# Quarter sums by accumulating DMAs, shift dots on VectorE and filters beside the first stage's last projections: one DiT layer on one core

## Chip, core and metric

The program runs on one core of a Trainium2 chip. The metric is the device time of one execution in microseconds (us). TensorE (PE) multiplies, PEld loads its weights, VectorE (DVE) and ScalarE (ACT) do element work, GpSimd (POOL) does element work and issues DMAs of its own queue, SyncE (SP) issues all other DMAs.

## What is computed

One layer of a diffusion transformer on 512 latent and 256 context tokens of width 1024, all in fp32. `m` and `mc` are nine vectors each, from the conditioning `c` and `c_ctx`:

```python
m = jnp.split((jax.nn.silu(c) @ mod_w[l] + mod_b[l])[:, None, :], N_MOD, axis=-1)
mc = jnp.split((jax.nn.silu(c_ctx) @ mod_w[l] + mod_b[l])[None, None, :], N_MOD, axis=-1)
h = half_ffn(h, m[0], m[1], m[2], ffn_w_gate[l, 0], ffn_w_up[l, 0], ffn_w_down[l, 0])
hc = half_ffn(hc, mc[0], mc[1], mc[2], ffn_w_gate[l, 0], ffn_w_up[l, 0], ffn_w_down[l, 0])
n = modulate(rms_norm(h), m[3], m[4])
nc = modulate(rms_norm(hc), mc[3], mc[4])
...
s_fw, s_bw = context_states(nc, w_in[l], lb_all[l])
...
out, _, _ = token_mixers(n, s_fw, s_bw, hyena_kernels(n_lat, *filt_w), *mix_w)
h = h + m[5] * out
h = half_ffn(h, m[6], m[7], m[8], ffn_w_gate[l, 1], ffn_w_up[l, 1], ffn_w_down[l, 1])
return rms_norm(h) * final_norm_w
```

`half_ffn` is a gated feed-forward network (hidden width 2816) on the normed input, shifted and scaled by two of the vectors. `token_mixers` projects with `w_in`, runs a gated linear recurrence in four heads and two long convolutions ("Hyena"), whose filters a small network makes, and projects back.

## The kernel before

Every fp32 operand of a matmul is split into a rounded high part and a low rest (`split`: a CAST on ACT, a subtraction on DVE or POOL), and each product is three matmuls (high by high, low by high, high by low).

**First stage** (`ffn0`, the first `half_ffn`, latents and context together). The 22 tiles of the hidden width are worked in five groups (`GROUPS0`: 4, 4, 4, 4 and 6 tiles); below they are groups 0 to 4. Group 0 multiplies plainly. Before it can work on the context, `shifts` must make the shift columns `m0` of the latents and the context: for each of eight tiles of `mod_w` two dots over 512 elements for the latents and one over 1024 for the context. Groups 1 to 4 use a seven-product scheme for 2x2 blocks (`quads0`): the 512-column quarters `a11, a12, a21, a22` of two weight tiles and four sums of them, `s1 = a21+a22`, `s2 = s1+a11`, `s3 = a11+a21`, `s4 = a12+s2`, are split and multiplied in the order a11, s2, s3, s1, a12, a22, s4 (in PE's names p1, p6, p7, p5, p2, p4, p3). Two tiles of gate and up weights make two such "quads", 18 in all. After its products each group multiplies with `w_d` for eight column tiles (the down part); the partial results of groups 0 to 3 are summed in DRAM, group 0 with stores, the others with accumulating DMAs of POOL's queue (`y_dram`, `yc_dram`). The last group's down part (`ps_dl` for latents, `ps_dc` for the context) adds them up with the residual.

**Background.** `bg` runs beside groups 0 to 4, a step at a time (`adv(bg)`, two in each quad, one at each column tile of a down part). `mod_steps` makes the other modulation vectors from 56 tiles of `mod_w` of 512 KB, two buffers in turn: tile n+1 can be loaded only when the dots of tile n-1 are done. The first 24 tiles are heavy (two dots over 512 and one over 1024), the other 32 light (one dot over 1024).

**Mixers.** After the first stage, 52 projection tiles (`fill_all`) are the fill of PE. Generators with long chains on DVE and ACT, `context_norm`, `filters` (four), `convs` (four halves, `e` forward and `j` back transform) and the heads, are run against the fill by `Clock.run`, which by hand-given costs (us of PE, us of chain) decides which piece is recorded next.

**What sets the order.** Weights are loaded along a list (`plan`), some tiles being held for a second use (`hold`). The recorded program then goes through a scheduler which reorders instructions on each engine (`schedule_with_timeline_sim=True`). SP, POOL, DVE, ACT and PE each work in order: an instruction that waits holds up all behind it on its engine.

Of the kernel before, what the change touches and what calls it, by code (L numbers as in the profile page):

```python
# [10 lines left out]
F32 = mybir.dt.float32  # L11
# [84 lines left out]
def layer_kernel(ctx: ExitStack, tc: tile.TileContext, a: dict, out: bass.AP):  # L96
# [26 lines left out]
        return mx.tile([P] + dims, dt, tag="c4", name=name, bufs=8)  # L123

    def c2(name, dims, dt=F32):
        return mx.tile([P] + dims, dt, tag="c2", name=name, bufs=15)

    def c1(name, dims, dt=F32):
        return mx.tile([P] + dims, dt, tag="c1", name=name, bufs=6)
# [5 lines left out]
    def load(dst, src):  # L135
        nc.sync.dma_start(out=dst, in_=src)
# [8 lines left out]
    def raw_tile(name):  # L145
        return wp.tile([P, 1024], F32, tag="wraw", name=name, bufs=3)
# [5 lines left out]
    for g, (f0, f1) in enumerate(GROUPS0):  # L152
        if g == 0:
            gu = [(a[w][0, ft], 1024) for ft in range(f0, f1) for w in ("wg", "wu")]
            plan += hold(gu[:6], [RING] * 3 + [ONE8, RES2, TWO4]) + gu[6:]
        else:
            plan += [(a[w][0, ft], a[w][0, ft + 1], QUAD0) for ft in range(f0, f1, 2) for w in ("wg", "wu")]
        down = [(a["wd"][0, dm, :, f0 * P:f1 * P], (f1 - f0) * P) for dm in range(KT)]
        plan += hold(down, [RING] * 3 + [ONE8] * 2 + [RES2] + [RING] * 2) + down[0:3] if g == len(GROUPS0) - 1 else down
# [78 lines left out]

    def quads0(src0, src1):

        raws = []
        for src in (src0, src1):
            raws.append(raw_tile("wraw"))
            load(raws[-1], src)
        (a11, a12), (a21, a22) = (r.rearrange("p (h c) -> h p c", h=2) for r in raws)

        def total(x, y):
            t = c2("qs", [512])
            V.tensor_tensor(out=t, in0=x, in1=y, op=ALU.add)  # L249
            return t  # L250

        def both(x, eng=V):
            w = ("whi", "wlo")[wstate["slot"]]
            wstate["slot"] ^= 1
            t = wp.tile([P, 2, 512], F32R, tag=w, name=w, bufs=3)
            split(t[:, 0], t[:, 1], x, eng)
            return t[:, 0], t[:, 1], None

        yield both(a11, G)
        s1 = total(a21, a22)  # L260
        s2 = total(s1, a11)
        yield both(s2)
        yield both(total(a11, a21))
        yield both(s1)
        yield both(a12, G)
        yield both(a22, G)
        yield both(total(a12, s2))
# [117 lines left out]
    def dot(out_, raw, vec, res):  # L385
        return V.scalar_tensor_tensor(out=out_, in0=raw, scalar=1.0, in1=vec, op0=ALU.mult, op1=ALU.mult, accum_out=res)  # L386

    m_part = const.tile([P, KT], F32, name="m_part")

    def mod_steps():  # L390
        raw = [c4("wmod", [1024]) for _ in range(2)]
        tiles = [(j, dm) for j in range(2, 9) for dm in range(KT)]

        def fetch(i):
            if i < len(tiles):
                load(raw[i % 2], a["mod_w"][8 * tiles[i][0] + tiles[i][1]])

        fetch(0)
        yield
        for n, (j, dm) in enumerate(tiles):  # L400
            fetch(n + 1)
            col = j * 8 + dm
            r = raw[n % 2]
            if j < 5:
                junk = c2("junk", [512])
# [190 lines left out]

    def scale_columns(h):

        row = mx.tile([2, 512], F32, tag="c2", name="mrow", bufs=15)
        A.copy(row, p_scale[h][0:2, :])  # L600
        p_ = ps("ps_mt")
        for k in range(4):
# [4 lines left out]

    p_scale = []

    def pool_dot(raw, res):  # L610

        G.tensor_tensor(out=raw, in0=raw, in1=cvb[1], op=ALU.mult)
        A.activation(raw, raw, AF.Identity, accum_out=res)

    def shifts(kts):
        for kt in kts:
            junk = c2("junk", [512])
            for h, res in enumerate((m0[:, kt, 0:1], m_part[:, kt:kt + 1])):
# [289 lines left out]
    def ffn0():  # L908
        for gi, (f0, f1) in enumerate(GROUPS0):
            ml, mc = [], []  # L910
            if gi == 0:
                kept = [weights(6 - i) for i in range(6)]
                early = [ps("ps_gl") for _ in range(4)]
                for kt in range(KT):
                    if kt == 1:
                        accc = squares(hc, range(KT), c1, C, V)
                    if kt == 2:
                        shifts(range(4))
                    if kt == 5:
# [61 lines left out]
            if gi < len(GROUPS0) - 1:  # L981
                for dm in range(KT):
# [10 lines left out]
                continue  # L993

            def residual0(h_, y, p_, m, dm):
                V.tensor_tensor(out=y, in0=p_, in1=y, op=ALU.add)
                V.scalar_tensor_tensor(out=h_, in0=y, scalar=m[:, 16 + dm:17 + dm], in1=h_, op0=ALU.mult, op1=ALU.add)

            for _ in bg:
                pass  # L1000
            acc = norm["lat"]
            kept = []
            hl2 = [c8("hl", [4, L]) for _ in range(2)]
            yl = [c8("yl", [4, L]) for _ in range(2)]
            hc2, yc = (c8(x, [KT, C]) for x in ("hc", "yc"))
            for dm in range(0, KT, 2):
                i, ks = dm // 4, slice(dm % 4, dm % 4 + 2)
                load(hl2[i][:, ks], x0_dram[:, dm:dm + 2])
                load(yl[i][:, ks], y_dram[:, dm:dm + 2])
            load(hc2, a["ctxT"])  # L1010
            load(yc, yc_dram)
            nhi, nlo = (Halves([c8(x, [4, L], F32R) for _ in range(2)]) for x in ("nhi", "nlo"))
            for dm in range(KT):
                pl = ps("ps_dl")
                kept.append(weights(min(2, KT - dm)))
                down(kept[dm], lx, [pl])
                residual0(hk(hl2, dm), hk(yl, dm), pl, m_lat, dm)
                sq_add(acc, hk(hl2, dm), dm, c2, L)
                store(h_dram[:, dm], hk(hl2, dm))
            accc = norm["ctx"]  # L1020
            nl = norm_steps(acc, hl2, LS, nhi, nlo, m_lat, 3, 4, c2)
            for n, dm in enumerate((6, 7, 3, 4, 5, 0, 1, 2)):
                pc = ps("ps_dc")
                prefetch(1 if n == 0 else 2)
                down(weights() if n >= 5 else kept[dm], cx, [pc[:, 0:C]])
                if n >= 1:
                    adv(nl, 1 if n < 3 else 2)
                residual0(hc2[:, dm], yc[:, dm], pc[:, 0:C], m_ctx, dm)
                sq_add(accc, hc2[:, dm], n, c1, C)
# [135 lines left out]
            yield cost / 2, 1.4  # L1165

    def fill_all():
        for _ in range(52):
            prefetch()
            while not chosen:  # L1170
# [567 lines left out]
```

## Time and profile before

| | |
|---|---|
| device time, median of 3 runs (range) | 1596.77 us (1595.14 to 1599.26) |
| the profiled execution: its time, its span | 1599.4 us, 1597.4 us |
| mean granted clock of TensorE | 0.965 |
| busy PE, DVE, ACT, POOL | 1473.6, 1190.6, 634.5, 473.4 us |
| moved by DMA | 209.60 MB |

The span runs from the first instruction to the last. A busy share is an average over stages that have different limits, so the stages are read one by one: which engine is full there, and what PE waits for.

### The profile page before, as it was taken

The page shows a single profiled execution, that of the slowest core. Times are in us where ns is not written, and L with a number is a line of the kernel's source. Part 1 is how long each engine was busy: PE and PEld are TensorE (multiplying, and loading weights), DVE is VectorE, ACT ScalarE, POOL GpSimd, SP SyncE. Part 2 cuts the span into 40 slices and gives each one's busy share as a digit, 9 for nine tenths or more (in the row PEclk, how much of TensorE's full clock was granted, in tenths as well). Part 3 has the DMA queues.
Part 4 walks back from the last instruction along what each step waited for, and adds up shares of the span by engine and source line. Part 5 has one row for each costly group of instructions (what it writes and reads, how often), then busy time and mean ns, then how long its engine had stood idle before and what let it go on. Part 6 is the DMA issues. An engine that isn't in the chain of part 4 may idle for free.

```text
span 1597.4 us, 22680 instructions
## 1 busy us (share of the span) xinstructions
PE 1473.6 (92%) x8560; PEld 1312.8 (82%) x8560; DVE 1190.6 (75%) x1833; ACT 634.5 (40%) x1141; POOL 473.4 (30%) x350
## 2 busy tenths in 40 slices
PE   8779887999999999999999958998798999999997
PEld 4578886988989988887778847887688899989897
DVE  6768995986868968665447888777466678869687
ACT  5344332343434445434232423444433344535353
POOL 1221534445545510135754111211232011302020
PEclk9989998999999999999999989998799999999998
DMA  9306338449393183435333541114423042322422
GB/s 386 102 21 225 131 119 216 139 130 253 115 262 100 50 298 108 140 104 185 119 122 126 171 157 62 45 49 145 161 93 116 14 118 89 105 92 97 122 72 87
DMA packets 81805, 209.60 MB, mean 131 GB/s; under 512 B 9179, under 2 KB 22239, under 8 KB 81056
## 3 DMA queue, kind: packets, MB, share of 16 engines
q1 hardware_dynamic: 71856, 193.18, 36.0%
q0 software_dynamic: 8256, 13.78, 4.3%
q8 instruction: 67, 1.10, 0.3%
q10 hardware_dynamic: 1584, 1.20, 0.2%
q14 instruction: 42, 0.34, 0.1%
HBM read 175.88 MB, written 32.24 MB: 130 GB/s over the span
## 4 chain that ended last, share of the span: by engine, by line
PE 59%; DVE 22%; DMA 7%; issue 6%; ACT 3%; POOL 1%; SPq 0%; ACTq 0%; DVEq 0%; POOLq 0%
PE ps_w L310 5%; PE ps_w L313 5%; PE ps_w L311 5%; PE ps_p L313 4%; PE ps_p L310 4%; PE ps_p L311 4%; PE ps_dl L310 3%; PE ps_dl L311 3%; PE ps_dl L313 3%; DMA wmod<-in_mod_w 3%; DVE wlo L143 2%; DVE junk L386 2%; DVE wmod L386 2%; DVE qs L249 2%; DVE whi L143 2%
## 5 line engine op out<-in xcount | busy, mean ns | idle before, releaser
L142 ACT CAST whi<-wraw 128x512 fp32r<-128x512 f32 (+2 forms) x187 | 151.4, 810 | 299.1 <-issue 78.4
L143 DVE TENSOR_TENSOR wlo<-wraw,whi 128x1024 fp32r<-128x1024 f32 (+2 forms) x114 | 124.6, 1095 | 57.4 <-ACT whi L142 55.1
L310 PE MATMUL ps_w<-nhi,whi 128*128 128x512 f32 x352 | 143.5, 408 | 0.0
L313 PE MATMUL ps_w<-nhi,wlo 128*128 128x512 f32 x352 | 140.0, 398 | 3.7 <-DVE wlo L143 3.7
L311 PE MATMUL ps_w<-nlo,whi 128*128 128x512 f32 x352 | 140.1, 398 | 0.0
L313 PE MATMUL ps_dl<-mid,wlo 128*128 128x512 f32 (+1 forms) x318 | 122.2, 387 | 0.2 <-DVE wlo L143 0.2
L311 PE MATMUL ps_dl<-mid,whi 128*128 128x512 f32 (+1 forms) x318 | 122.1, 386 | 0.0
L310 PE MATMUL ps_dl<-mid,whi 128*128 128x512 f32 (+1 forms) x318 | 121.0, 388 | 0.2 <-ACT mid L142 0.2
L143 POOL TENSOR_TENSOR wlo<-wraw,whi 128x1024 fp32r<-128x1024 f32 x19 | 51.0, 2684 | 232.5 <-ACT whi L142 189.0
L1564 POOL TENSOR_TENSOR u<-p,res 128x512 f32<-128x512 f32 x18 | 33.0, 1833 | 283.9 <-ACT p L1559 140.6
L386 DVE SCALAR_TENSOR_TENSOR wmod<-wmod,cvb 128x1024 f32<-128x1024 f32 x56 | 73.5, 1313 | 24.6 <-DMA wmod<-in_mod_w 24.3
L313 PEld LDWEIGHTS ps_w<-nhi,wlo 128*128 128x128 f32 x352 | 66.9, 190 | 16.6 <-DVE wlo L143 4.2
L310 PEld LDWEIGHTS ps_w<-nhi,whi 128*128 128x128 f32 x352 | 67.3, 191 | 15.1
L311 PEld LDWEIGHTS ps_w<-nlo,whi 128*128 128x128 f32 x352 | 67.2, 191 | 11.5
L142 ACT CAST whi<-qs 128x512 fp32r<-128x512 f32 x72 | 44.3, 619 | 78.8 <-DVE qs L249 40.2
L143 DVE TENSOR_TENSOR whi<-qs,whi 128x512 fp32r<-128x512 f32 x72 | 67.4, 947 | 4.6 <-ACT whi L142 4.3
L143 DVE TENSOR_TENSOR wlo<-qs,wlo 128x512 fp32r<-128x512 f32 x72 | 58.1, 813 | 16.6 <-ACT wlo L142 15.9
L142 ACT CAST wlo<-qs 128x512 fp32r<-128x512 f32 x72 | 43.9, 619 | 66.3 <-DVE qs L249 41.5
L310 PEld LDWEIGHTS ps_dl<-mid,whi 128*128 128x128 f32 x318 | 59.5, 188 | 12.3 <-ACT mid L142 0.7
L143 POOL TENSOR_TENSOR wlo<-wraw,wlo 128x512 fp32r<-128x512 f32 x27 | 48.2, 1785 | 65.7 <-ACT wlo L142 58.3
L313 PEld LDWEIGHTS ps_dl<-mid,wlo 128*128 128x128 f32 x318 | 60.0, 189 | 7.5 <-DVE wlo L143 0.4
L311 PEld LDWEIGHTS ps_dl<-mid,whi 128*128 128x128 f32 x318 | 59.9, 188 | 7.3 <-DVE mid L143 0.2
(533 smaller groups left out, 4929.2 us busy)
## 6 DMA issues: line engine op xcount, KB each, us to landing
wmod<-in_mod_w SPq DMA_DIRECT2D x56, 512.0 KB, 3.5
wraw<-in_wg SPq DMA_DIRECT2D x44, 512.0 KB, 3.4
wraw<-in_wu SPq DMA_DIRECT2D x44, 512.0 KB, 3.4
wraw<-in_w_in SPq DMA_DIRECT2D x44, 512.0 KB, 3.3
wraw<-in_wd SPq DMA_DIRECT2D x35, 384.0 KB, 3.5
wraw<-in_wd SPq DMA_DIRECT2D x40, 256.0 KB, 3.0
wm<-in_mod_w SPq DMA_DIRECT2D x16, 512.0 KB, 10.2
y_dram<-yt POOLq DMA_DIRECT2D x24, 256.0 KB, 9.2
```

What stands on the lines that cost most here:

```text
L142: A.copy(hi, x)
L143: return eng.tensor_tensor(out=lo, in0=x, in1=hi.bitcast(F32), op=ALU.subtract)
L249: V.tensor_tensor(out=t, in0=x, in1=y, op=ALU.add)
L310: PE.matmul(o, whi, xhi, start=first, stop=False)
L311: PE.matmul(o, whi, xlo, start=False, stop=False)
L313: PE.matmul(o, wlo, xhi, start=False, stop=last)
L386: return V.scalar_tensor_tensor(out=out_, in0=raw, scalar=1.0, in1=vec, op0=ALU.mult, op1=ALU.mult, accum_out=res)
L1564: G.tensor_tensor(out=u57, in0=p57, in1=res[:, 1:2].broadcast_to([P, 2, 256]), op=ALU.add)
```

## The change

1. **Quarter sums.** In `quads0`, s1 and s3 are no longer made by DVE. SP loads one of the two terms into a tile `qs`, and a DMA of POOL's queue adds the other onto it (`accum_op=add`). a21 alone is no longer loaded; the loads of a quad are five of 256 KB on SP's queue and two accumulating ones of 256 KB on POOL's, in place of two of 512 KB.
2. **Shift dots.** All eight context dots of `shifts` are on DVE; before, six were a product on POOL and a sum on ACT. The Silu of the conditioning vectors `cvb` and the norm factors of the context (`rstd_steps`) are recorded earlier.
3. **Background tiles.** Of the first 48 tiles, heavy and light ones take turns.
4. **Last down part.** `ffn0_end` is a generator that is itself fill; `filters` run beside it from its first piece, `context_norm` once it is done. Five of its eight weight tiles are loaded twice, before three.
5. The scratch tile `junk` of the dots has a place of its own; the ring of 512-element tiles has 14 places, before 15.

```diff
     def quads0(src0, src1):
...
-        (a11, a12), (a21, a22) = (r.rearrange("p (h c) -> h p c", h=2) for r in raws)
+        a11, a12 = raw_tile("wraw").rearrange("p (h c) -> h p c", h=2)
+        k0, k1 = slice(0, 512), slice(512, 1024)
+        load(a11, src0[:, k0])
+        s1, s3 = (c2("qs", [512]) for _ in range(2))
+        for t, x, y in ((s1, src1[:, k0], src1[:, k1]), (s3, src0[:, k0], src1[:, k0])):
+            load(t, x)
+            nc.gpsimd.dma_start(out=t, in_=y, accum_op=ALU.add)
+        load(a12, src0[:, k1])
+        a22 = raw_tile("wraw")[:, 0:512]
+        load(a22, src1[:, k1])
...
-        s1 = total(a21, a22)
         s2 = total(s1, a11)
         yield both(s2)
-        yield both(total(a11, a21))
+        yield both(s3)
         yield both(s1)
...
         tiles = [(j, dm) for j in range(2, 9) for dm in range(KT)]
+        tiles = [tiles[i // 2 if i % 2 == 0 else 24 + i // 2] for i in range(48)] + tiles[48:]
...
-    def pool_dot(raw, res):
-
-        G.tensor_tensor(out=raw, in0=raw, in1=cvb[1], op=ALU.mult)
-        A.activation(raw, raw, AF.Identity, accum_out=res)
-
     def shifts(kts):
...
-            if kt in (0,1,3,4,5,7):
-                pool_dot(shift_w[kt], m0[:, kt, 1:2])
-            else:
-                dot(shift_w[kt], shift_w[kt], cvb[1], m0[:, kt, 1:2])
+            dot(shift_w[kt], shift_w[kt], cvb[1], m0[:, kt, 1:2])
...
-                    if kt == 5:
-                        for _ in rstd_steps([accc], C, "rc", rx):
-                            pass
+                    if kt == 2:
+                        stats = rstd_steps([accc], C, "rc", rx)
+                        adv(stats)
+                    if kt == 4:
+                        adv(stats, 2)
...
+    def ffn0_end(lx, cx):
...
+            store(h_dram[:, dm], hk(hl2, dm))
+            yield 4.1, 2.2
...
     def fill_all():
+        yield from ffn0_end(*ends)
         for _ in range(52):
...
-    ck.run([context_norm(), filters()], fill, lambda i: True, 2)
+    ck.run([filters(), context_norm()], fill, lambda i: i == 0 or "mixers" in state, 2)
```

**DVE ahead of the context's first products** (`wm` is a tile of `mod_w`, `m_part` the second halves of the latents' dots, `rr` the context's norm factors). Before:

```order
L143 TENSOR_TENSOR wkeep<-wraw,wkeep 128x1024 x2
L460 RECIPROCAL rr<-rr 128x2
L143 TENSOR_TENSOR wkeep<-wraw,wkeep 128x1024
L386 SCALAR_TENSOR_TENSOR junk,m_193<-wm_332,cvb 128x512
L386 SCALAR_TENSOR_TENSOR junk,m_193<-wm_334,cvb 128x512
```

Now:

```order
L143 TENSOR_TENSOR wkeep<-wraw,wkeep 128x1024 x2
L390 SCALAR_TENSOR_TENSOR junk,m_194<-wm_333,cvb 128x512
L390 SCALAR_TENSOR_TENSOR junk,m_part<-wm_333,cvb 128x512
L465 RECIPROCAL rr<-rr 128x2
L390 SCALAR_TENSOR_TENSOR wm_333,m_194<-wm_333,cvb 128x1024
L390 SCALAR_TENSOR_TENSOR junk,m_194<-wm_335,cvb 128x512
L467 TENSOR_TENSOR dg<-ident,rr 128x256
L143 TENSOR_TENSOR wkeep<-wraw,wkeep 128x1024
```

The first dots stand ahead of the context's norm factors, and each tile's context dot follows its two latent dots on the same engine.

**SP at the start of group 3** (its first quad reads two tiles of `in_wg`, the next two of `in_wu`). Before:

```order
L136 DMA wraw_3304<-in_wg 128x1024
L136 DMA wmod_1109<-in_mod_w 128x1024
L136 DMA wraw_3306<-in_wg 128x1024
L136 DMA wmod_1108<-in_mod_w 128x1024
L136 DMA wraw_3405<-in_wu 128x1024
```

Now:

```order
L136 DMA wraw_3277<-in_wg 128x512 x2
L136 DMA wmod_1095<-in_mod_w 128x1024
L136 DMA wraw_3286<-in_wg 128x512
L136 DMA wmod_1096<-in_mod_w 128x1024
L136 DMA wraw_3382<-in_wu 128x512 x2
L136 DMA wmod_1095<-in_mod_w 128x1024
L136 DMA wmod_1096<-in_mod_w 128x1024
L136 DMA qs_3279<-in_wg 128x512
L136 DMA qs_3280<-in_wg 128x512
```

The second tile of weights stood ahead of two background loads that stand ahead of s1's and s3's first terms now.

**DVE at the same place.** Before:

```order
L386 SCALAR_TENSOR_TENSOR wmod_1109,m_lat_96<-wmod_1109,cvb_328 128x1024
L249 TENSOR_TENSOR qs_3311<-wraw_3306 128x512
L249 TENSOR_TENSOR qs_3313<-qs_3311,wraw_3304 128x512
L143 TENSOR_TENSOR wlo_3315<-qs_3313,wlo_3315 128x512
L386 SCALAR_TENSOR_TENSOR wmod_1108,m_lat_96<-wmod_1108,cvb_328 128x1024
```

Now:

```order
L390 SCALAR_TENSOR_TENSOR wmod_1096,m_lat_96<-wmod_1096,cvb_329 128x1024
L254 TENSOR_TENSOR qs_3291<-qs_3279,wraw_3277 128x512
L254 TENSOR_TENSOR qs_3361<-wraw_3277,qs_3291 128x512
L143 TENSOR_TENSOR wlo_3293<-qs_3291,wlo_3293 128x512
L390 SCALAR_TENSOR_TENSOR junk_146,m_lat_96<-wmod_1095,cvb_329 128x512
```

s2 (`qs_3291`) follows the same light dot; what it reads, `qs_3279`, is now written by a load and an accumulating DMA.

**PE in the convolutions**, around the first two back transforms. Before:

```order
L313 MATMUL ps_e<-zhi,ft 128x256
L310 MATMUL ps_j<-it,ys 128x256
L311 MATMUL ps_j<-it,ys 128x256
L310 MATMUL ps_j<-it,ys 128x256
L311 MATMUL ps_j<-it,ys 128x256
L310 MATMUL ps_e<-zhi,ft 128x256
```

Now:

```order
L317 MATMUL ps_w<-nhi,wlo 128x512
L314 MATMUL ps_w<-nhi,whi 128x512
L315 MATMUL ps_w<-nlo,whi 128x512
L317 MATMUL ps_w<-nhi,wlo 128x512
L314 MATMUL ps_j<-it,ys 128x256
L315 MATMUL ps_j<-it,ys 128x256
```

The first back transform stood straight behind the forward transform that feeds it; now 114 matmuls of fill (`ps_w`) stand between the two. The second half's `j` stands straight behind its `e` in both.

## Rows read from the trace of the kernel before

**Rows 1.** The page's first part: busy time and share of each engine.
```profile
PE 1473.6 (92%) x8560; PEld 1312.8 (82%) x8560; DVE 1190.6 (75%) x1833; ACT 634.5 (40%) x1141; POOL 473.4 (30%) x350
```
**Rows 2.** Windows: stretch, length, busy PE, PEld, DVE, ACT, POOL (instructions), clock, DMA share, GB/s.
```profile
75.00:100.00 25.00, 11.98 (x76) 11.99 (x77) 13.93 (x27) 7.75 (x18) 8.96 (x6) 0.62 0.05 17
159.00:236.00 77.00, 68.02 (x374) 64.41 (x372) 76.83 (x123) 28.32 (x57) 34.98 (x23) 1.00 0.40 130
...
264.00:349.00 85.00, 69.58 (x374) 65.99 (x373) 76.51 (x113) 28.87 (x58) 36.96 (x25) 0.94 0.47 145
349.00:376.00 27.00, 27.00 (x156) 23.57 (x155) 13.55 (x25) 10.13 (x23) 13.44 (x15) 1.00 0.90 241
376.00:447.00 71.00, 68.06 (x375) 66.38 (x375) 61.95 (x83) 29.35 (x58) 37.58 (x26) 0.98 0.53 162
...
474.00:570.00 96.00, 93.21 (x511) 90.78 (x510) 79.94 (x110) 46.59 (x88) 50.05 (x39) 0.98 0.34 102
570.00:604.00 34.00, 33.65 (x149) 27.39 (x148) 22.82 (x34) 10.68 (x17) 0.00 (x0) 1.00 0.80 299
```
**Rows 3.** PE's waits: matmul, what it waited for, us in total, times, longest.
```profile
PE ps_j L310 <- ACT ys L142: 22.1, 3, 13.9
PE ps_gc L310 <- ACT bh L142: 18.2, 1, 18.2
PE ps_p L310 <- ACT wlo L142: 11.0, 1, 11.0
...
PE ps_w L313 <- DVE wlo L143: 3.7, 1, 3.7
```
**Rows 4.** DVE's timeline, 51 to 88 us: start, us, instruction, idle time before.
```profile
51.43 0.17 DVE L460 RECIPROCAL rr<-rr 128x2 f32<-128x2 f32 x1 [7.83 <-ACT rr L459]
...
54.74 0.69 DVE L386 SCALAR_TENSOR_TENSOR junk<-wm,cvb 128x512 f32<-128x512 f32 x1 [1.15 <-ACT cvb L663]
...
58.75 2.89 DVE L386 SCALAR_TENSOR_TENSOR junk<-wm,cvb 128x512 f32<-128x512 f32 x1
...
67.72 1.21 DVE L386 SCALAR_TENSOR_TENSOR wm<-wm,cvb 128x1024 f32<-128x1024 f32 x1
...
69.87 1.27 DVE L628 SCALAR_TENSOR_TENSOR mt<-hc,m,rc 128x256 f32<-128x256 f32 x3
...
87.56 0.17 DVE L932 TENSOR_TENSOR m<-m,sm 128x16 f32<-128x16 f32 x1 [3.48 <-ACT wm L613]
```
**Rows 5.** Groups by line, whole span: busy, mean ns, idle time before.
```profile
L249 DVE TENSOR_TENSOR qs<-wraw 128x512 f32<-128x512 f32 x36 | 39.6, 1101 | 4.5 <-DMA wraw<-in_wg 4.1 <-DMA wraw<-in_wu 0.5
...
L991 POOL DMA_DIRECT2D y_dram<-yt x24 | 24.5, 1021 | 55.1 <-ACT yt L987 54.7
```
**Rows 6.** Groups by line, DVE in 159 to 236 us.
```profile
L386 DVE SCALAR_TENSOR_TENSOR junk<-wmod,cvb 128x512 f32<-128x512 f32 x18 | 18.2, 1011 | 0.1
L386 DVE SCALAR_TENSOR_TENSOR wmod<-wmod,cvb 128x1024 f32<-128x1024 f32 x10 | 13.6, 1364 | 0.0
```
**Rows 7.** DMA queues (packets, MB, share), then issues: KB each, median us to landing.
```profile
q1 hardware_dynamic: 71856, 193.18, 36.0%
q0 software_dynamic: 8256, 13.78, 4.3%
...
wraw<-in_wg SPq DMA_DIRECT2D x44, 512.0 KB, 3.4
...
y_dram<-yt POOLq DMA_DIRECT2D x24, 256.0 KB, 9.2
...
k_dram<-te POOLq DMA_DIRECT2D x8, 256.0 KB, 3.8
```
**Rows 8.** Timeline of SP's queue at the start of group 3.
```profile
375.30 5.44 SPq L136 DMA_DIRECT2D wmod<-in_mod_w  x2
```
**Rows 9.** Timeline of PE at the start of group 3.
```profile
378.57 0.45 PE L310 MATMUL ps_p<-tt,wlo 128*128 128x386 f32 x1
...
384.18 0.69 PE L310 MATMUL ps_p<-tt,whi 128*128 128x386 f32 x1 [2.83 <-ACT whi L142]
```

More of the change, by code (lines that the diff above doesn't have):

```diff
@@ L125, in c2 @@
     def c2(name, dims, dt=F32):
-        return mx.tile([P] + dims, dt, tag="c2", name=name, bufs=15)
+        return mx.tile([P] + dims, dt, tag="c2", name=name, bufs=14)
     def c1(name, dims, dt=F32):
@@ L158, in layer_kernel @@
         down = [(a["wd"][0, dm, :, f0 * P:f1 * P], (f1 - f0) * P) for dm in range(KT)]
-        plan += hold(down, [RING] * 3 + [ONE8] * 2 + [RES2] + [RING] * 2) + down[0:3] if g == len(GROUPS0) - 1 else down
+        plan += hold(down, [RING] * 5 + [RES2] + [RING] * 2) + down[0:5] if g == len(GROUPS0) - 1 else down
     plan += [None] * 52
@@ L239, in quads0 @@
     def quads0(src0, src1):
[L241 to L244, printed above, removed]
-        (a11, a12), (a21, a22) = (r.rearrange("p (h c) -> h p c", h=2) for r in raws)
+        a11, a12 = raw_tile("wraw").rearrange("p (h c) -> h p c", h=2)
[8 more added lines that the diff above has]
+        load(a22, src1[:, k1])
         def total(x, y):
@@ L386, in dot @@
         return V.scalar_tensor_tensor(out=out_, in0=raw, scalar=1.0, in1=vec, op0=ALU.mult, op1=ALU.mult, accum_out=res)
+    junk = const.tile([P, 512], F32, name="junk")
     m_part = const.tile([P, KT], F32, name="m_part")
@@ L404, in mod_steps @@
             if j < 5:
-                junk = c2("junk", [512])
                 for h, res in enumerate((m_lat[:, col:col + 1], m_part[:, dm:dm + 1])):
@@ L597, in scale_columns @@
     def scale_columns(h):
-        row = mx.tile([2, 512], F32, tag="c2", name="mrow", bufs=15)
+        row = mx.tile([2, 512], F32, tag="c2", name="mrow", bufs=14)
         A.copy(row, p_scale[h][0:2, :])
@@ L608, in layer_kernel @@
     p_scale = []
-    def pool_dot(raw, res):
-        G.tensor_tensor(out=raw, in0=raw, in1=cvb[1], op=ALU.mult)
-        A.activation(raw, raw, AF.Identity, accum_out=res)
     def shifts(kts):
         for kt in kts:
-            junk = c2("junk", [512])
             for h, res in enumerate((m0[:, kt, 0:1], m_part[:, kt:kt + 1])):
@@ L659, in layer_kernel @@
     shift_w = rows(range(4), "wm0")
+    for i in range(2):
+        tc.keep_in_program_order(A.activation(cvb[i], cvb[i], AF.Silu))
     prefetch(6)
     shift_w += rows(range(4, KT), "wm0")
-    for i in range(2):
-        tc.keep_in_program_order(A.activation(cvb[i], cvb[i], AF.Silu))
     for i in range(2):
@@ L992, in ffn0 @@
                     adv(bg)
[L993 to L1029, printed above, removed]
@@ L1030, in ffn0, with residual0 @@
-            adv(nl, 8)
-        return nhi, nlo, hc2
+        return lx, cx
+    nhi = nlo = chi = clo = hc2 = lat_x = None
+    def ffn0_end(lx, cx):
+        nonlocal nhi, nlo, chi, clo, hc2, lat_x
+        def residual0(h_, y, p_, m, dm):
+            V.tensor_tensor(out=y, in0=p_, in1=y, op=ALU.add)
+            V.scalar_tensor_tensor(out=h_, in0=y, scalar=m[:, 16 + dm:17 + dm], in1=h_, op0=ALU.mult, op1=ALU.add)
+        for _ in bg:
+            pass
+        acc = norm["lat"]
+        kept = []
+        hl2 = [c8("hl", [4, L]) for _ in range(2)]
+        yl = [c8("yl", [4, L]) for _ in range(2)]
+        hc2, yc = (c8(x, [KT, C]) for x in ("hc", "yc"))
+        for dm in range(0, KT, 2):
+            i, ks = dm // 4, slice(dm % 4, dm % 4 + 2)
+            load(hl2[i][:, ks], x0_dram[:, dm:dm + 2])
+            load(yl[i][:, ks], y_dram[:, dm:dm + 2])
+        load(hc2, a["ctxT"])
+        load(yc, yc_dram)
+        nhi, nlo = (Halves([c8(x, [4, L], F32R) for _ in range(2)]) for x in ("nhi", "nlo"))
+        for dm in range(KT):
+            pl = ps("ps_dl")
+            kept.append(weights(min(2, KT - dm)))
+            down(kept[dm], lx, [pl])
+            residual0(hk(hl2, dm), hk(yl, dm), pl, m_lat, dm)
+            sq_add(acc, hk(hl2, dm), dm, c2, L)
+            store(h_dram[:, dm], hk(hl2, dm))
+            yield 4.1, 2.2
+        accc = norm["ctx"]
+        nl = norm_steps(acc, hl2, LS, nhi, nlo, m_lat, 3, 4, c2)
+        for n, dm in enumerate((6, 7, 5, 0, 1, 2, 3, 4)):
+            pc = ps("ps_dc")
+            prefetch(1 if n == 0 else 2)
+            down(weights() if n >= 3 else kept[dm], cx, [pc[:, 0:C]])
+            if n >= 1:
+                adv(nl, 1 if n < 3 else 2)
+            residual0(hc2[:, dm], yc[:, dm], pc[:, 0:C], m_ctx, dm)
+            sq_add(accc, hc2[:, dm], n, c1, C)
+            yield 2.1, 2.5
+        adv(nl, 8)
+        lat_x = (nhi, nlo, LS)
+        chi, clo = (c8(x, [KT, C], F32R) for x in ("chi", "clo"))
+        zt["hi"] = c8("zhi", [4, 512], F32R)
+        zt["lo"] = c8("zlo", [4, 512], F32R)
+        state["mixers"] = True
@@ L1033, in layer_kernel @@
     norm = {"lat": [], "ctx": []}
     ck = Clock()
-    nhi, nlo, hc2 = ffn0()
-    lat_x = (nhi, nlo, LS)
-    chi, clo = (c8(x, [KT, C], F32R) for x in ("chi", "clo"))
+    ends = ffn0()
     deferred = []
@@ L1185, in need @@
         flush(True)
-    zt["hi"] = c8("zhi", [4, 512], F32R)
-    zt["lo"] = c8("zlo", [4, 512], F32R)
-    zhi, zlo = zt["hi"], zt["lo"]
     def context_norm():
@@ L1206, in layer_kernel @@
     ftab = forward_table()
-    ck.run([context_norm(), filters()], fill, lambda i: True, 2)
+    ck.run([filters(), context_norm()], fill, lambda i: i == 0 or "mixers" in state, 2)
+    zhi, zlo = zt["hi"], zt["lo"]
     inverse_table(0)
```

## Prediction

> **What bounds the kernel now.** The first view is the share of each engine: PE is busy for 92% of the span, DVE for 75% [rows 1], so at most some 120 us can be won, in the places where PE is not at work. The second is PE's waits: the reader is to see three of weight. `ps_gc`, the context's first products, waits 18.2 us once for the shift columns; `ps_j`, the convolutions' back transforms, 22.1 us in three waits, the longest 13.9; `ps_p`, the products of the quads, 11.0 us at the start of group 2 [rows 3]. The third is the table of windows, which tells what each stage is short of. In group 1's products DVE is busy for 76.83 of 77 us and PE for 68.02: DVE is the bound. In group 2's it is nearly so (76.51 of 85), in groups 3 and 4 it is not (61.95 of 71, 79.94 of 96). The down parts run PE full with the DMA engines at 0.90 [rows 2].
>
> **Part 1, shift columns: -10 us.** Before, DVE stands at the RECIPROCAL until 51.43 us, begins the dots at 54.74, and after its own last dot waits 3.48 us for the dots of POOL and ACT; the columns are summed at 87.56 [rows 4]. While POOL multiplied, a half dot took 2.89 us in place of 0.69 [rows 4]. Now the first two half dots stand ahead of the RECIPROCAL, which PE's order holds where it was. Behind it DVE has 14 half dots of 0.69 (9.7), eight of 1.21 (9.7), eight norm products at 0.42 (three take 1.27; 3.4) and the splits of the same eight, which I put at the same 3.4, and two small ones (1.5): 27.7 us by durations, some 2 less since neighbours overlap. 51.6 + 25.9 = 77.5, ten before 87.56. Bounds: -13 if loads and norm factors are never late, -6 if tiles 4 to 7, whose loads wait for the buffers of 0 to 3, are. PE restarts at the lower clock either way (0.62 over that window [rows 2]); two more ACT table loads cost nothing, since ACT idles there.
>
> **Part 2, quarter sums and background tiles: +14 us in all.** Four things meet.
>
> *Relief.* 36 adds of 1101 ns leave DVE, 39.6 us [rows 5], eight of them, 8.8 us, in each of groups 1 to 3. In group 1 four of some nine heavy tiles turn light: a heavy one is two dots of 1011 ns and one of 1364, a light one the latter alone [rows 6], so 4 x 2.0 = 8. DVE's work there falls from 76.8 to 60 us. In groups 2 and 3 the heavy tiles come back: +8 each, against -8.8. Nothing is won there.
>
> *Group starts.* s2, the second product's weights, now hangs on a chain: load, POOL's issue, accumulation. At group 3 SP issues a background load at 375.30, when DVE's light dot is over [rows 8]; s1's first term stands behind just such a load, so at 375.9; landing 3.4 [rows 7] gives 379.3, POOL's issue 1.0 [rows 5] 380.3. What the accumulation takes no row tells. A plain transfer of the size on POOL's queue lands in 3.8, an accumulating one into DRAM, in the saturated down parts, in 9.2 [rows 7]. Below 3.8 nothing speaks for it. I take 6: the products' DMA share is half of the down parts' (0.53 against 0.90 [rows 2]), but the transfer reads its target too and begins among the last sums into DRAM. So 386.3, add and split some 1.7, 388. PE wants the weights at 378.57 [rows 9] and stands 9.5 us, where it stood 2.83 at 381 to 384 [rows 9]: +7 (+4.5 to +10), and the clock falls behind it (0.98 over the 71 us [rows 2] is 1.4 us lost already): +1.5. DVE waits too, s2 being its next instruction, with two dots and all other splits queued behind.
>
> *Second quads.* Their s1 load stands behind a background load that waits for the third dot of the tile, behind s3's split in DVE's order: +1.5 each. Later quads have slack: from s4 of two quads back the chain is 1.2 + 3.4 + 1.0 + 6, 11.6 us, and s2 is due about one quad (some 14 us) later: nothing at 6 us.
>
> *Sum by group.* Group 1: DVE's 60 us of work, 10 of waiting at its start, 2 at the second quad: 72 against 77, -5. Group 2: work unchanged; its start has the 11.0 us wait already [rows 3], +3. Group 3: +7 +1.5 +1.5 -2 (lighter waits), +8. Group 4: the same, +8. Together +14; with both ends of the accumulation 0 to +40.
>
> A rule of the Trainium skill stands against the 6 us: *DMA: Bandwidth & Descriptors*, section "Anatomy of one DMA", gives about 2.0 us plus bytes over 436 GB/s for a DMA of POOL's queue, 2.6 for 256 KB as an estimate. By it the sum would be some 20 us lower. No run here shows 2.6: the nearest row has 3.8, and 9.2 where it accumulates [rows 7], so the row decides.
>
> **Part 3, convolutions: -11 us.** Of the three `ps_j` waits [rows 3] the first goes, since 114 matmuls of 512 columns of fill (some 26 us; 149 take 33.65 [rows 2]) now stand ahead of the first back transform. The second half's is exposed in full, and not behind the first one's `j` as before: I take 13 of the 22.1 as left, -9, and -2 of lower clock. Bounds: 0 (the wait moves) to -16.
>
> **Part 4, filters beside the last down part: +3 us.** PE is full there, 33.65 of 34 us, DMA at 0.80 [rows 2]. The filters' matmuls now stand in PE's order among `ps_dl`, their tables and weights in SP's among `hl`, `yl` and two more 256 KB tiles of `w_d`, all in a stretch that is short of DMA: from 0 to +10. The two extra splits lie beside full PE. The one place less in the ring of tiles costs nothing as long as loads wait for background tiles first.
>
> **Sum.** -10 +14 -11 +3 = -4, and -4 for the 3.7 us that the first projection waits for its split [rows 3], since filter matmuls now stand ahead of it: -8. The profiled execution took 1599.4 us for a span of 1597.4 and stands 2.6 above the median of the runs, 1596.77; so 1599.4 - 8 - 2.6, about 1589 us. Anything within 0.3% (4.8 us) of 1596.8 can't be told from no change.
>
> **Rivals.** *A, late accumulations* (slower): they land after 9.2 us, as into DRAM. Four starts and four second quads lose 3.2 us more each, 26 in all, some 3 of them hidden: 1612. For it: the only accumulating row; the DMA bytes of a quad rise from 1 to 1.75 MB. Against it: half the DMA load. It decides from 7 us of landing on, where eight places cost 8 us and the sum is nought. Beside it the same page of the Trainium skill, *DMA: Bandwidth & Descriptors*, section "Issuing engines are not separate DMA queues", says that all DMAs share 16 engines, and a second issuer saves issue time alone. The rows bear it out in part. Queue q0, which is POOL's, needed 4.3% of the engines' span for 13.78 MB, q1 36.0% for 193.18 [rows 7], 5.0 against 3.0 us per MB; 9.4 MB more on the first and 4.7 on the second are 61 us of all engines over 18 quads, 3.4 us in each, with shares of 0.34 to 0.53 before [rows 2]. That fills, but does not bound.
>
> *B, quick accumulations*: they land after 3.8 us; the starts lose 2.2 less each (9), the second quads nothing (6): 1574. For it: the plain row. Against it: the target is read too.
>
> *C, the two moves of fill bring nothing*: PE stands behind filter weights in the DMA-bound stretch for 6 us more, and the convolutions' wait moves to the second half at nearly full length (+7): 1602. For it: DMA at 0.80 [rows 2] and PE working in order. Against it: 26 us of fill ahead of the first transform.
>
> **Chances and range.** The forecast 0.42 (own range 1580 to 1598, of it 0.25 faster, 0.12 same, 0.05 slower); A 0.27 (0.02, 0.02, 0.23); B 0.17, all faster; C 0.14 (0.03, 0.07, 0.04). Faster 0.47, same 0.21, slower 0.32. From 1566 (B with shift columns 3 us better and its starts at the bound) to 1618 (A with the filters at their upper bound) some 0.8 of the cases lie.
>
> **What would show it.** Right: DVE ends the shift columns at 77 to 78 us and POOL has no `wm` product; `qs` transfers of POOL's queue land in about 6 us; PE stands about 10 us behind the first product of groups 1 to 4, for s2; group 1's products take 72 us, group 3's near 79; one long `ps_j` wait of about 13 us is left; `ps_dl` runs without a wait over 3 us. Wrong: a landing under 4 or over 8 us, waits for s2 in third and later quads, group 1 still full of DVE work, or `ps_j` waiting 20 us again.

## The result, and the profile after

The changed kernel takes 1642.38 us (median of 4 runs, 1641.29 to 1650.18), the one before 1598.01 in the same comparison: ratio 1.0287, 95% interval 1.0249 to 1.0326. It is slower by some 44 us where 8 us less was forecast, and outside the range. The profiled execution took 1642.2 us for a span of 1640.4.

The page's first part shows an odd thing to begin with: DVE has less work, as meant, and PE is busy for longer though it does the same matmuls [rows 1].

```profile
PE 1489.6 (91%) x8560; PEld 1328.0 (81%) x8560; DVE 1151.7 (70%) x1811; ACT 631.7 (39%) x1133; POOL 467.8 (29%) x380
```

To find where the 43.0 us of span came from, I cut both executions on PE's timeline where group 1's first `ps_p`, each next group's first `ps_p` and the last down part's first `ps_dl` stand:

| stretch | before, us | after, us | difference |
|---|---|---|---|
| to group 1's products | 159.1 | 148.6 | -10.5 |
| group 1, products and down part | 104.9 | 111.3 | +6.4 |
| group 2 | 112.4 | 121.4 | +9.0 |
| group 3 | 98.1 | 121.2 | +23.1 |
| group 4, products | 95.9 | 118.6 | +22.7 |
| last down part to the end | 1027.0 | 1019.3 | -7.7 |

The down parts of groups 1 to 3 take 33.6 to 33.7 us, before 33.7 to 34.7. So the loss lies in the products of the quads, all of it: they grow from 70.0, 78.6, 64.2 and 95.7 us to 77.5, 87.6, 87.4 and 118.4, by some 62. The windows of these products (columns as in [rows 2]; groups 1 to 4, then the last down part) tell two things:

```profile
148.00:226.00 78.00, 64.12 (x340) 62.89 (x339) 56.80 (x85) 28.60 (x56) 37.24 (x31) 0.91 0.58 158
260.00:347.00 87.00, 66.94 (x334) 65.44 (x333) 54.82 (x85) 28.68 (x56) 39.37 (x33) 0.86 0.61 158
381.00:469.00 88.00, 65.12 (x340) 63.58 (x340) 57.66 (x88) 28.50 (x56) 39.96 (x33) 0.88 0.61 159
502.00:621.00 119.00, 100.30 (x513) 95.20 (x512) 69.53 (x99) 46.71 (x89) 56.34 (x49) 0.90 0.52 131
621.00:692.00 71.00, 67.64 (x372) 56.87 (x371) 55.06 (x83) 29.96 (x48) 15.38 (x15) 0.95 0.56 196
```

The windows of [rows 2] for groups 1 to 3 reach 6 to 7 us into the down parts; that of group 1's products alone, before, is

```profile
159.00:229.00 70.00, 61.22 (x337) 58.67 (x336) 69.90 (x109) 28.12 (x56) 34.98 (x23) 1.00 0.38 123
```

DVE is no longer the bound of group 1: 56.80 of 78 us, where it had been full. And the granted clock is 0.86 to 0.91 in all four, where it had been 0.94 to 1.00: behind the long waits PE works at the lower of its two levels (1.2 in place of 2.4 GHz) for a while, so these waits are paid for twice. PE's waits (columns as in [rows 3]) say what it stood for:

```profile
PE ps_p L314 <- ACT wlo L142: 55.2, 9, 12.9
PE ps_p L314 <- ACT whi L142: 20.0, 7, 5.0
...
PE ps_gc L314 <- ACT bh L142: 8.3, 1, 8.3
PE ps_j L314 <- ACT ys L142: 8.1, 1, 8.1
PE ps_w L317 <- DVE wlo L143: 6.8, 2, 3.5
...
PE ps_p L317 <- DVE wlo L143: 3.6, 5, 1.2
...
PE ps_w L753 <- ACT w3h L742: 1.6, 1, 1.6
```

Two of the three large waits of before have shrunk as forecast, `ps_gc` from 18.2 to 8.3 us and `ps_j` from 22.1 to 8.1 [rows 3]. The quads' `ps_p` has grown to 78.8 us. Before it had 33.1, since beside the 11.0 of [rows 3] there were three more rows:

```profile
PE ps_p L313 <- DVE wlo L143: 8.4, 10, 1.4
PE ps_p L313 <- DVE whi L143: 7.1, 6, 2.3
PE ps_p L310 <- ACT whi L142: 6.6, 3, 2.8
```

Of these, 75.3 us now and 29.6 before are in the first stage, the rest in the second feed-forward network. ACT is only the last link there: its CAST waits for s2, and s2 for the quarter sum. The chain can be followed at the start of group 3, the place of [rows 8, 9]. DVE's timeline:

```profile
380.57 1.22 DVE L390 SCALAR_TENSOR_TENSOR wmod<-wmod,cvb 128x1024 f32<-128x1024 f32 x1 [1.30 <-DMA wmod<-in_mod_w]
...
395.06 0.69 DVE L254 TENSOR_TENSOR qs<-qs,wraw 128x512 f32<-128x512 f32 x1 [13.25 <-DMA qs<-in_wg]
```

SP's queue:

```profile
379.30 2.86 SPq L136 DMA_DIRECT2D wmod<-in_mod_w  x2
382.27 0.86 SPq L136 DMA_DIRECT2D qs<-in_wg  x2
```

POOL, and PE:

```profile
390.92 0.86 POOL L247 DMA_DIRECT2D qs<-in_wg  x1 [7.92 <-DMA qs<-in_wg]
392.04 0.86 POOL L247 DMA_DIRECT2D qs<-in_wg  x1 [0.26 <-issue]
```

```profile
396.45 0.69 PE L314 MATMUL ps_p<-tt,wlo 128*128 128x386 f32 x1 [12.90 <-ACT wlo L142]
```

As forecast, SP's two loads stand behind a background load that waits for DVE's light dot, and DVE then has nothing but s2 to go on with. The sizes differ. From SP's issue of the first term at 382.3 to the start of POOL's at 390.9 it took 8.6 us, where I had 3.4 for the landing; POOL's issue and the accumulation together from 390.9 to 395.1, 4.1 us, not 7. DVE stood 13.25 us, PE 12.90. The DMA issues (KB each, median us to landing) show that the accumulation itself was no worse than I took it:

```profile
y_dram<-yt POOLq DMA_DIRECT2D x24, 256.0 KB, 8.5
qs<-in_wg SPq DMA_DIRECT2D x18, 256.0 KB, 5.1
qs<-in_wg POOLq DMA_DIRECT2D x18, 256.0 KB, 4.8
qs<-in_wu SPq DMA_DIRECT2D x18, 256.0 KB, 3.7
qs<-in_wu POOLq DMA_DIRECT2D x18, 256.0 KB, 4.9
```

It lands in 4.8 to 4.9 us in SBUF, where the one into DRAM takes 8.5 in the same run. What I had at nothing is the later quads. In group 3's fourth quad the second of the two background loads at 424.04 waits until 432.9 for a dot of DVE; behind it stand two weight loads, and the quad's own sums go out at 441.77:

```profile
424.04 9.19 SPq L136 DMA_DIRECT2D wmod<-in_mod_w  x2
437.13 0.33 SPq L136 DMA_DIRECT2D wraw<-in_wu  x1
441.34 0.33 SPq L136 DMA_DIRECT2D wraw<-in_wd  x1
441.77 1.11 SPq L136 DMA_DIRECT2D qs<-in_wu  x2
```

The weight loads do not wait for dots. Each wants one of the three weight buffers (`wraw`), and the quad before has to free it: the first with a split of POOL, the second with s4 on DVE. The CAST of that split stands on ACT behind the CAST of s3, which waits for an accumulation:

```profile
432.90 0.62 ACT L142 CAST whi<-qs 128x512 fp32r<-128x512 f32 x1 [7.61 <-DMA qs<-in_wg]
...
434.98 0.62 ACT L142 CAST wlo<-wraw 128x512 fp32r<-128x512 f32 x1
```

```profile
435.68 1.43 POOL L143 TENSOR_TENSOR wlo<-wraw,wlo 128x512 fp32r<-128x512 f32 x1 [0.28 <-ACT wlo L142]
```

```profile
440.63 0.68 DVE L254 TENSOR_TENSOR qs<-wraw,qs 128x512 f32<-128x512 f32 x1
```

In nine of the ten third and later quads a weight load is the last thing that SP waits for ahead of the sums' loads. Group 4 shows it plainly: its last background load goes out at 501.55, before its products begin, and between 505 and 621 us SP's queue waits for

```profile
SPq L136 <- POOL wlo L143: 44.3, 3, 15.4
SPq L136 <- POOL whi L143: 42.5, 4, 14.2
SPq L136 <- DVE qs L254: 6.3, 2, 3.5
```

Back in group 3's fourth quad, DVE has a heavy tile ahead of s2; one dot takes 4.05 us in place of 1.2 while POOL issues the accumulations and works on tiles of its own. The dot cost little here: the accumulation, issued at 446.97, took 4.0 us, and s2 began 0.6 us behind its landing. PE stands another 5 us:

```profile
447.61 4.05 DVE L390 SCALAR_TENSOR_TENSOR wmod<-wmod,cvb 128x1024 f32<-128x1024 f32 x1
...
451.59 0.68 DVE L254 TENSOR_TENSOR qs<-qs,wraw 128x512 f32<-128x512 f32 x1
```

```profile
454.73 0.69 PE L314 MATMUL ps_p<-tt,whi 128*128 128x386 f32 x1 [5.04 <-ACT whi L142]
```

The four group starts have 43.9 of the first stage's 75.3 us (6.5, 11.9, 12.9, 12.7); the other 31.4 are spread over later quads, the sign of being wrong that the prediction had named ("waits for s2 in third and later quads").

### The profile page after: what moved, and what is told of

The parts are those of the page before. It is cut to its first block, busy times and chain, and to the rows that moved or that the text cites. A ratio compares the mean times of both kernels' runs of the same rounds, so it can differ in the third digit from the quotient of the medians.

```text
span 1640.4 us, 22788 instructions
## 1 busy us (share of the span) xinstructions
PE 1489.6 (91%) x8560; PEld 1328.0 (81%) x8560; DVE 1151.7 (70%) x1811; ACT 631.7 (39%) x1133; POOL 467.8 (29%) x380
## 4 chain that ended last, share of the span: by engine, by line
PE 60%; DMA 14%; DVE 12%; issue 7%; POOL 4%; ACT 3%; SPq 1%; ACTq 0%; POOLq 0%; DVEq 0%
DMA qs<-in_wg 5%; PE ps_w L314 5%; PE ps_w L317 5%; PE ps_w L315 5%; PE ps_dl L314 4%; PE ps_p L314 4%; PE ps_p L317 4%; PE ps_dl L317 4%; PE ps_p L315 4%; PE ps_dl L315 4%; DMA wmod<-in_mod_w 4%; DMA qs<-in_wu 3%; DVE wlo L143 2%; PE ps_s L1370 1%; PE ps_gl L314 1%
## 5 line engine op out<-in xcount | busy, mean ns | idle before, releaser
L317 PE MATMUL ps_dl<-mid,wlo 128*128 128x512 f32 (+1 forms) x330 | 128.4, 391 | 0.0
L315 PE MATMUL ps_dl<-mid,whi 128*128 128x512 f32 (+1 forms) x330 | 128.1, 389 | 0.0
L314 PE MATMUL ps_dl<-mid,whi 128*128 128x512 f32 (+1 forms) x330 | 126.8, 392 | 0.0
L143 POOL TENSOR_TENSOR wlo<-wraw,whi 128x1024 fp32r<-128x1024 f32 x19 | 47.2, 2485 | 248.4 <-ACT whi L142 244.2
L390 DVE SCALAR_TENSOR_TENSOR wmod<-wmod,cvb 128x1024 f32<-128x1024 f32 x56 | 79.2, 1416 | 19.5 <-DMA wmod<-in_mod_w 19.1
L314 PE MATMUL ps_p<-tt,wlo 128*128 128x386 f32 x72 | 31.1, 431 | 55.2 <-ACT wlo L142 55.2
L143 DVE TENSOR_TENSOR wlo<-qs,wlo 128x512 fp32r<-128x512 f32 x72 | 63.1, 882 | 14.1 <-ACT wlo L142 13.8
L314 PEld LDWEIGHTS ps_dl<-mid,whi 128*128 128x128 f32 x330 | 62.5, 190 | 12.8 <-ACT mid L142 0.2
L254 DVE TENSOR_TENSOR qs<-qs,wraw 128x512 f32<-128x512 f32 x18 | 14.3, 796 | 82.1 <-DMA qs<-in_wg 61.9
L315 PEld LDWEIGHTS ps_dl<-mid,whi 128*128 128x128 f32 x330 | 62.7, 190 | 7.9
```

The costliest lines, as they stand in the source:

```text
L143: return eng.tensor_tensor(out=lo, in0=x, in1=hi.bitcast(F32), op=ALU.subtract)
L314: PE.matmul(o, whi, xhi, start=first, stop=False)
L315: PE.matmul(o, whi, xlo, start=False, stop=False)
L317: PE.matmul(o, wlo, xhi, start=False, stop=last)
```

## Experiments

Two theories stood at the start. **C, the chain**: load, POOL's issue, accumulation and s2 are too long for the quads, wherever they stand. **T, the turns**: the heavy tiles that now stand ahead of s2 in groups 2 to 4 hold DVE up. Undoing one, the other or both tells them apart, and doing the sums alone is the test from the other side.

**Sums back on DVE** (the `quads0` of before in the changed kernel):

```diff
-        for t, x, y in ((s1, src1[:, k0], src1[:, k1]), (s3, src0[:, k0], src1[:, k0])):
-            load(t, x)
-            nc.gpsimd.dma_start(out=t, in_=y, accum_op=ALU.add)
+        s1 = total(a21, a22)
...
+        yield both(total(a11, a21))
```

> The changed kernel with the quarter sums back on DVE (loads of two whole tiles, four adds). Theory C (the chain load, POOL issue, accumulation, s2 makes PE stand in every quad and its clock fall behind it): the 78.8 us that ps_p waits in the changed kernel fall to some 35, and the rest of the change is left, the shift columns 10 us and the convolutions 14 us: 1570 to 1580 us. Rival T (the heavy tiles that now stand ahead of s2 in groups 2 to 4 are what holds DVE): little comes back, 1620 to 1635 us.

Measured: 1583.11 us (1580.75 to 1583.81), ratio to before 0.9910 (0.9889 to 0.9931). PE's waits in the quads of the first stage, added up from its timeline, are 23.6 us, against 75.3 in the changed kernel and 29.6 before. 59 us come back; the time is 3 us over theory C's range.

**Tiles in their old order**, sums still by DMA:

```diff
-        tiles = [tiles[i // 2 if i % 2 == 0 else 24 + i // 2] for i in range(48)] + tiles[48:]
```

> The changed kernel with the background tiles in their old order, 24 heavy ones first; the sums stay with the DMAs. Theory C: the chain stays, so the long waits at the group starts stay, 10 to 13 us each; only the waits of the fourth quads (5 us in group 3) go: 1630 to 1645 us. Rival T: groups 3 and 4 fall back to some 75 and 98 us of products: 1600 to 1610 us.

Measured: 1647.57 us (1644.94 to 1652.95), ratio 1.0321 (1.0292 to 1.0349). Nothing comes back, so rival T falls. The time is 2.6 us over theory C's range, and the waits are 73.9 us.

**Both undone**:

> Both undone: what is left is the shift dots and the filters beside the last down part. Both theories: 1575 to 1585 us, group 1's products again full of DVE work at some 77 us. If the filters' new place costs more than the 3 us that the prediction put down, 1590 or more.

Measured: 1577.69 us (1576.27 to 1580.02), ratio 0.9880 (0.9859 to 0.9901), waits 21.7 us. This is faster than the kernel before by 1.2%, and than the sums on DVE with turns by 5.4 us, their ranges apart: the turns, with which group 1 gains 3.0 us of products (67.4 against 70.4), lose 7.6 in group 3 (71.2 against 63.6).

**Sums by DMA alone**, in the kernel before (its `quads0` replaced by that of the change):

> The kernel before with the accumulating sums as its only change. Theory C: the loss without the gains, 1640 to 1660 us, long ps_p waits at each group start though the tiles stand in their old order. Rival T: no heavy tile has moved, so 1590 to 1605 us.

Measured: 1654.37 us (1653.32 to 1655.88), ratio 1.0357 (1.0332 to 1.0381). The products of the four groups grow to 79.1, 92.8, 82.5 and 114.1 us. Theory C holds from both sides. What the waits cost beside themselves is seen from the second and third run, whose one difference is the sums. The last line of a table of windows over the four groups' products adds up the busy time; first with the sums by DMA, then on DVE:

```profile
sum 371.00, PE 296.74 PEld 285.39 DVE 244.37 ACT 132.12 POOL 174.49; mean PE 74.18 PEld 71.35 DVE 61.09 ACT 33.03 POOL 43.62
```

```profile
sum 302.00, PE 280.31 PEld 272.86 DVE 273.00 ACT 131.88 POOL 159.01; mean PE 70.08 PEld 68.21 DVE 68.25 ACT 32.97 POOL 39.75
```

Of some 70 us, 52 are waits (73.9 less 21.7) and 16.4 are PE's own time: the granted clock of the four windows is 0.87 to 0.93 with the sums by DMA and 0.95 to 0.98 without.

Next, what in the chain is too long: the accumulation, or a load that comes late on SP?

**First terms only** (old order of tiles; the sums lack their second terms):

```diff
             load(t, x)
-            nc.gpsimd.dma_start(out=t, in_=y, accum_op=ALU.add)
```

> The changed kernel with the tiles in their old order, in which s1 and s3 are only loaded: the accumulating DMAs of the quads are left out, so the sums lack their second terms; order, buffers and the places of the loads stay. It stands between 1647.6 us (with them) and 1577.7 (sums on DVE). Theory C1 (the accumulating transfer itself, POOL's issue and 4.8 us of landing, makes the chain too long): 1575 to 1590 us, group starts without long waits. Theory C2 (the loads come too late, behind background loads on SP): the group starts keep 7 us of their 12, 1605 to 1625 us.

Measured: 1588.61 us (1588.14 to 1591.86), ratio 0.9951 (0.9936 to 0.9966). The time is that of theory C1, 59 of the 70 us gone; but not by its picture, for three of the four group starts keep waits of 8.1 to 9.1 us:

```profile
PE ps_p L313 <- ACT wlo L142: 27.8, 4, 9.1
```

Four waits, one for each start, hold 27.8 of the 31.9 us. There the late load is the larger part, in all other quads the accumulating DMA (its issue, its transfer and what it does to others, together). Both theories had a piece each.

**Sums recorded a quad ahead** (old order of tiles). Loads and accumulations are issued from a function that the quad before calls, for a group's first quad a tile of `w_d`:

```diff
+        sums[n] = [c2("qs", [512]) for _ in range(2)]
+        for t, x, y in ((sums[n][0], src1[:, k0], src1[:, k1]), (sums[n][1], src0[:, k0], src1[:, k0])):
+            load(t, x)
+            nc.gpsimd.dma_start(out=t, in_=y, accum_op=ALU.add)
...
         load(a22, src1[:, k1])
+        quad_sums(n + 1)
...
             load(raw[:, :cols], src)
+            quad_sums(wstate["next"] + 2)
```

> The changed kernel with the tiles in their old order; the loads and accumulations of a quad's s1 and s3 are recorded one quad ahead, those of a group's first quad two tiles of w_d ahead. If only the start of the chain is late, the waits vanish and 39.6 us of adds are off DVE for good: 1565 to 1580 us. If what holds them is SP's and POOL's order behind the background loads: 1600 to 1630 us.

Measured: 1593.70 us (1589.26 to 1595.70), ratio 0.9975 (0.9962 to 0.9988). 54 of the 70 us come back by an earlier start alone, and the waits are 26.5 us. The rest, 16 us over the sums on DVE, does not, so neither expectation was met.

**The same with turns**:

> The same with heavy and light tiles in turns. If the chain is hidden, DVE's work in group 1 falls by 17 us and turns pay for themselves: 1560 to 1575 us. If turns only put heavy dots ahead of s2 in groups 2 to 4: 5 to 10 us more than without them.

Measured: 1597.07 us (1593.15 to 1602.40), ratio 1.0006 (0.9992 to 1.0021), no difference from before. The medians of the two stand 3.4 us apart, but the ranges overlap. The turns don't pay for themselves here either.

**Shift dots alone**, in the kernel before (no `pool_dot`, Silu and `rstd_steps` earlier):

> The kernel before with the shift dots' part as its only change (all eight context dots on DVE, Silu and norm factors of the context earlier). Forecast of the prediction: ps_gc waits 8 in place of 18.2 us, 10 us off, 1586 to 1590 us. If DVE's extra dots only move the wait elsewhere: 1595 or more.

Measured: 1584.39 us (1581.12 to 1587.14), ratio 0.9926 (0.9909 to 0.9943). `ps_gc` waits 5.3 us, not 8:

```profile
PE ps_gc L310 <- ACT bh L142: 5.3, 1, 5.3
```

Here five half dots stand ahead of the RECIPROCAL, in the changed kernel, with `junk` in a place of its own, two. Whether the scratch tile makes the difference is the first question below.

Three tries to better the 1577.69 us follow.

**Scratch tile of the shift dots from the ring** (the run with both undone, with `junk = c2("junk", [512])` in `shifts`):

> Sums on DVE, tiles in their old order (1577.7 us), and the scratch tile of the shift dots from the ring of 512-element tiles again, one for each tile of mod_w. With one scratch place only two half dots stand ahead of the RECIPROCAL, in the run of the shifts alone five do, and PE's wait is 5.3 us in place of 8.3: 3 us off, 1574 to 1576 us. If the scratch place is not what orders the dots: 1577 to 1579 us.

Measured: 1577.25 us (1576.08 to 1578.14), ratio 0.9872 (0.9858 to 0.9885). The wait falls from 8.3 to 5.9 us and five half dots stand ahead of the RECIPROCAL, so the scratch tile did order them. Group 1's products begin 3.4 us sooner (147.0 against 150.4), but the median moves by 0.4 us only. Group 4 is done 4.2 us sooner; the last down part with its filters takes 74.1 us in place of 71.8, 1.4 us of the lead are left through most of the projections, and by `ps_pa` it is gone. Why, stays open.

**Heavy tiles in the down parts** (in the run just before):

```diff
+        downs = [*range(0, 7), *range(15, 23), *range(31, 39), 47]
+        heavy, light = iter(tiles[:24]), iter(tiles[24:])
+        tiles = [next(heavy if n in downs else light) for n in range(56)]
```

> The same, and 23 of the 24 heavy tiles set at the column tiles of the down parts, where DVE has room, and none in the quads of groups 1 and 2. If DVE's work bounds group 1's products (70.9 busy of 71 us): 5 to 8 us off there, 1567 to 1571 us. If PE's waits there hang on the order of splits and not on the sum of DVE's work: within 2 us of the run beside it.

Measured: 1579.32 us (1577.03 to 1580.69), ratio 0.9886 (0.9869 to 0.9902). Group 1's products fall from 70.6 to 64.8 us, so DVE's work did bound them; groups 3 and 4 take 6.3 and 5.3 us more. Why they do, with light tiles, stays open.

**s3 alone by DMA, a quad ahead** (in the run with the scratch tile from the ring):

> The first of the three with s3 alone by load and accumulating DMA, recorded a quad ahead; s1 and s2 stay on DVE. s3 is wanted one product later than s2 and nothing is made from it. If an accumulating DMA costs only where its landing is waited for: 18 adds less on DVE, 1570 to 1574 us. If it costs by its presence (POOL's issue, slower DVE beside it, DMA load): 1580 us or more.

Measured: 1581.83 us (1575.90 to 1582.18), ratio 0.9893 (0.9877 to 0.9909). 18 adds less bring nothing: a median 4.6 us above the run with all sums on DVE, though the ranges overlap.

The best versions found are the two with the sums on DVE, the tiles in their old order, the shift dots and the filters as in the change, 1577 to 1578 us, 1.2 to 1.3% under the kernel before.

## Why the prediction was wrong

The step that failed is "Later quads have slack", with "nothing at 6 us", and with it the relief of group 1, which was reckoned as if DVE's work and the start alone set the pace there. The products of the quads grew by some 62 us where the sum by group had +14. In the prediction's own terms:

| term | put at, us | measured, us |
|---|---|---|
| waits at the four starts (17.6 before) | 10 + 3 + 7 + 7 = +27 | 43.9, +26 |
| waits in all other quads (12.0 before); relief, second quads, lighter waits | -16 | 31.4, +19 |
| PE's own time, the clock | +3 | +16 |

- **Shift columns, -10**: right. The stretch to group 1 is 10.5 us shorter; DVE sums the columns at 75.9 us, forecast 77.5. Alone the part is worth more, 12.6 us by the medians.
- **Convolutions, -11**: right in mechanism, the exposed wait was smaller, 8.1 us and not 13, so -14.
- **Last down part with filters, +3**: about right. It takes 70.9 us with the filters' matmuls in it, with no wait over 2 us. PE is without work for 3.4 of 71 us there, 0.4 of 54 before; the row after is the last of the first table of windows above, the one before is

```profile
570.00:624.00 54.00, 53.58 (x315) 47.11 (x314) 40.34 (x62) 24.17 (x38) 2.76 (x2) 1.00 0.60 218
```

- **First projection, -4**: wrong. Its wait for the split did not go but became two, 6.8 us in place of 3.7 (`ps_w` above), at 696 and 704 us, behind the last down part. So of the -12 that parts 3 and 4 and this term had together, 7.7 came: -14, +3 and +3.
- **Relief**: "DVE's work there falls from 76.8 to 60 us" was read from a window that reaches 7 us into the down part; in the products alone DVE went from 69.9 of 70 us to 56.8 of 78. It was no use, since the chain took DVE's place as the bound.
- **Group starts**: the chain was named rightly, and that the waits' sum came out at +26 is luck: two terms were off in opposite ways. "landing 3.4" was the median over the whole span; at this place two terms, a background load and the last sums into DRAM were in flight together, and it was 8.6 us until POOL's issue, while issue and accumulation took 4.1 for 7. The unknown I had spent my care on, the landing of the accumulation, was 4.8 where I took 6, nearer to the low end. So rival A falls, on its own condition: the slowest accumulation of a sum took 7.7 us, none 9.2. Rivals B and C fall as well.
- **Later quads**: the slack was worked out from the length of the chain alone, as if SP, POOL and DVE were free when it wanted them. In fact SP's loads of the terms stand behind weight loads, and in groups 1 to 3 behind background loads too; the weight loads wait for a buffer that a split or s4 of an earlier quad frees, and these stand behind what waits for an accumulation: the queues close a ring, as followed above for one quad. The first-terms run shows that outside the group starts the accumulating DMA is what closes it, and the run with the sums a quad ahead that most of the price is its place in time. Which link holds longest, the weight buffers, the background loads or the order in which the scheduler put SP's loads, was not tested apart.
- **Clock**: "+1.5" for a start was counted for groups 3 and 4 alone, 3 us in all, and nothing for the later waits. PE's own time in the products grew by 16.4 us, from 280.1 to 296.5, and by as much between the two runs in the old order of tiles.
- **Turns**: put at 8 us less of DVE's work in group 1, and in groups 2 and 3 at 8 more, which the adds that left were to pay for. With the sums on DVE the turns cost 5.4 us. In group 3 DVE was busy for 64.60 of 71 us then, not full, and PE's waits there rose from 2.6 to 8.0 us; so it is not the sum of DVE's work alone, and what it is stays open.

The Trainium skill's rule from *DMA: Bandwidth & Descriptors*, section "Anatomy of one DMA", gives an estimated 2.6 us for a DMA of 256 KB on POOL's queue. The accumulating ones of the sums took 4.8 to 4.9, so this trace does not bear it out for them. Of plain ones the prediction named a row of 3.8 as the nearest; the trace before has two more of that size and queue, 2.8 (`k_dram<-to`) and 4.9 (`k_dram<-tw`), on both sides of it, so 3.8 was no lower bound. By the rule the forecast would have been lower still, and further off.

## What to carry to other kernels

A sum that a DMA makes is not off the path because its engine is idle: it turns one instruction into a chain of two transfers and an issue, which stands in two in-order queues and is waited for by a third. Before such a move, follow for one steady turn of the loop, and not only for its start, what each of the queues waits for ahead of it, buffers included; if the links form a ring, its length and not the busy time of an engine can set the pace. Recording the chain a whole turn earlier brought 54 of 70 us back here; leaving the adds on DVE brought back all of them.

## What the hardware showed beside that

- An accumulating DMA of 256 KB landed in 4.8 to 4.9 us (median) in SBUF and in 8.5 in DRAM, in one run. The two stand in different stages, with different DMA load, so how much is the target's is not told. Recorded a quad ahead, the same transfers took 8.5 and 6.2.
- Adds that left DVE took their full time with them. Between the two runs in the old order of tiles, with the sums on DVE and by DMA, DVE's busy time over the whole span fell from 1196.1 to 1159.5 us, by 36.6, and its adds in the quads from 69.1 to 32.3, by 36.8. The two lines of sums over windows above show 28.6 less, for they hold the products alone, and the longer products hold more of the other work. Single kinds of work did change: the background dots over 1024 went from 1307 to 1382 ns. The first row has the sums by DMA, the second on DVE:

```profile
L390 DVE SCALAR_TENSOR_TENSOR wmod<-wmod,cvb 128x1024 f32<-128x1024 f32 x56 | 77.4, 1382 | 21.7 <-DMA wmod<-in_mod_w 21.1
```

```profile
L386 DVE SCALAR_TENSOR_TENSOR wmod<-wmod,cvb 128x1024 f32<-128x1024 f32 x56 | 73.2, 1307 | 23.3 <-DMA wmod<-in_mod_w 23.0
```

- A scratch tile that nobody reads orders the work all the same: with one place for `junk` two half dots stood ahead of the RECIPROCAL, with a ring five, and PE's wait differed by 2.4 us (8.3 and 5.9).
